# A transformer trunk on one core: two branches' weight sums move to VectorE, the last sums in HBM are issued one per product

## The chip, the core and the metric

The kernel runs on one core of one Trainium2 chip. The metric is the device time of one execution in microseconds (us); less is better. Engines: TensorE (PE; PEld is its weight load), VectorE (DVE), ScalarE (ACT), GpSimd (POOL) and SyncE (SP). SP issues the loads into on-chip memory; GpSimd issues the transfers that add in HBM.

## The reference

Sequence 512, width 1024, all in float32. One layer:

```python
h = _rmsnorm(x, norm_mix[l])
p = h @ w_in[l]
u, v, bg, cg, xb, zc, gl = jnp.split(p, splits, axis=-1)
ya = _sgu(gelu(u), gelu(v), sgu_ln[l], sgu_w[l], sgu_b[l])
yb = bg * _causal_dwconv(cg * xb, conv_b_w[l])
yc = _pool_mixer(zc, pool_w[l], pool_scale[l])
g = jax.nn.sigmoid(gl).reshape(bn, s, N_BRANCH, D_MODEL)
merged = (g[:, :, 0] * (ya @ w_br_a[l])
          + g[:, :, 1] * (yb @ w_br_b[l])
          + g[:, :, 2] * (yc @ w_br_c[l]))
x = x + merged @ w_o[l]
h = _rmsnorm(x, norm_ffn[l])
a = _causal_dwconv(h @ w_up[l], ffn_conv_w[l])
ag, av = jnp.split(a, 2, axis=-1)
x = x + (jax.nn.silu(ag) * av) @ w_down[l]
```

and a last RMSNorm. `w_in` is 1024 x 6144 (its last 3072 columns are the three gates), each `w_br` 512 x 1024, `w_up` 1024 x 5632, `w_down` 2816 x 1024. The change concerns the three products with `w_br` ("branches") and the three with the gates' columns ("gates").

## The kernel before

Precision: every float32 operand is cut into a high and a low part (`split`: a copy on ScalarE, line 59, and a subtraction on VectorE, line 67; lines 63 and 64 with the sign turned), and each product is three matmuls of 128x512 (`mm3`, lines 81 to 83).

Stages, in order of time: the `v` projection; the other projections of `w_in` (`u`, `z`, `cg`, `xb`, `bg`; tiles `pu` to `pbg`); then three times a branch and its gate (`bx0`, `gx0`, ...); the output product (`po`); the up projection (`pug`, `puv`); the down projection (`dx`, ...); the end.

Branches and gates are computed by a scheme with seven products of half-size blocks in place of eight: with quarters b11, b12, b21, b22 of the weights, M1 and M3 use b11 and b22, M2 uses b21, and M5, M6, M7, M4 use the sums t1 = b11+b12, t2 = b22+t1, t3 = b12+b22, t4 = b21+t2. A branch product has 12 matmuls, a gate product 24.

The sums of the weights are made in HBM: `WeightSums.copy` issues four copies, `add` four transfers that add into the copies; t2 waits for t1, and t4 for t2. All stand on GpSimd's queue in the order written (`in_order`): branch 0's copies as soon as a part of the first weights has landed (`pool_waits_for(wv_raw[3], "begun")`), then GpSimd's centering of `v`, then branch 0's adds, gate 0's copies and adds, branch 1's, gate 1's, branch 2's, gate 2's. A branch's transfers are 0.5 MB each, a gate's 1 MB.

Weights reach the chip in pieces of 128x1024 (512 KB). `Raws` keeps at most four loads under way or unsplit (`cap` 4): each freed buffer starts the next load on SP's queue (line 106), in the order of use. `Pieces` cuts each into one of four ring slots (`ring_hi`, `ring_lo`), so that three pieces stand cut ahead of the one that TensorE reads; a piece feeds 12 matmuls. Before the stage of the branches the ring is fed by `Cols` with two loads for each projection block of 48 matmuls.

An automatic scheduler sets each engine's instruction order when the program is built; an engine then works in that order and waits where an operand isn't there. One such order matters at the start: ScalarE's cast of `pw_raw` (a small weight, loaded on SP's queue) stands ahead of the last cast of `hT`.

Of the kernel before, what the change touches and what calls it, by code (L numbers as in the profile page):

```python
# [11 lines left out]
ALU = mybir.AluOpType  # L12
# [14 lines left out]
def trunk_kernel(  # L27
# [4 lines left out]
    nc = tc.nc  # L32
# [99 lines left out]
    class WeightSums:  # L134
        def __init__(self, name, b11, b12, b21, b22):
            t1, t2, t3, t4 = self.t = [
                dram.tile([P, b11.shape[1], 528], F32, name=f"{name}_t{i + 1}")[:, :, :512] for i in range(4)]
            self.base = [(t1, b11), (t3, b12), (t2, b22), (t4, b21)]
            self.added = [(t1, b12), (t3, b22), (t2, t1), (t4, t2)]

            self.products = (("m1", b11), ("m5", t1), ("m6", t2), ("m2", b21), ("m7", t3), ("m3", b22), ("m4", t4))

        def copy(self, n=4):
            for t, w in self.base[:n]:
# [8 lines left out]

    NEGATIVE = ("m1", "m4")

    def add_seven(name, weights, pieces):
        for m, w in weights.products:
            n = w.shape[1]
            for q in range(0, n, 2):
                add_block(f"{name}_{m}_{q}", w[:, q:min(q + 2, n)], pieces,  # L160
                          split_negative if m in NEGATIVE else split)

    def add_block(name, view, pieces, cut):
        raws.add(name, view)
# [180 lines left out]
    def quarters(half, c0):  # L345
        return [half(k)[:, :, c0 + 512 * h:c0 + 512 * h + 512] for k in range(2) for h in range(2)]

    gate_sums = [WeightSums(f"g{i}", *quarters(lambda k: w_in_v[:, 4 * k:4 * k + 4], 3072 + 1024 * i))
                 for i in range(3)]
    branch_sums = [WeightSums(f"br{i}", *quarters(lambda k: w_br_q[i][k], 0)) for i in range(3)]  # L350

    def pool_waits_for(t, name):

        in_order(nc.gpsimd.tensor_copy(tiny(name, name), t[:, 0:1]))

    pool_waits_for(wv_raw[3], "begun")
    branch_sums[0].copy()

    nc.vector.memset(ones_r.bitcast(F32), 1.0)
    eps_t = const.tile([P, 1], F32, name="eps_t")  # L360
# [220 lines left out]
        v_mm(t, 7)  # L581
        v_gelu(t)
    v_center()
    for i in range(3):
        branch_sums[i].copy()
        branch_sums[i].add()
        gate_sums[i].copy()
        gate_sums[i].add()

    raws.live = 0  # L590
    blocks = Cols(col_blocks[:n_in], slots)
# [164 lines left out]

    pieces = Pieces(slots)
    for i in range(3):
        add_seven(f"br{i}", branch_sums[i], pieces)
        add_seven(f"g{i}", gate_sums[i], pieces)  # L760

    for h in range(2):
        for k in (4, 6, 0, 2):
# [99 lines left out]
    def of_quarter(kh, r):  # L863
        return lambda k, i: [h[:, 4 * kh + k, 256 * r + P * i:256 * r + P * i + P] for h in hT]
# [6 lines left out]
    nrstd1 = small.tile([P, NT], F32, tag="nrstd", name="nrstd1")  # L871
    nc.vector.tensor_scalar(nrstd1, rstd1, -1.0, None, op0=ALU.mult)

    def product(o, st, n, first, last=True):

        for q in range(0, n, 2):
            [w] = pieces.take()
            for k in range(q, q + 2):
                mv = [p[:, 512 * (k - q):512 * (k - q) + 512] for p in w]
                for r in range(2):  # L880
                    mm3(o[r], st(k, r), mv, first and k == 0, k == n - 1, more=not first)
# [7 lines left out]
    def banks(name):  # L889
        return [bank(f"{name}{r}") for r in range(2)]  # L890
# [3 lines left out]
    def gate(i, c):  # L894
        def sigmoid(t, s, src, scale=rstd1):
            nc.scalar.activation(s, src, AF.Sigmoid, scale=scale[:, t:t + 1])

        def weigh(t, h, s):
            if i == 0:
                tt(c[t][h], s, c[t][h], ALU.mult)  # L900
            else:
                tt(s, s, c[t][h], ALU.mult)
                tt(acc[t][h], acc[t][h], s, ALU.add)

        x = banks(f"gx{i}")
        product(x, of_quarter(0, 0), 4, True)
        m1 = copies(0, f"m1{i}", x)
        d = banks(f"gd{i}")
        product(d, of_form(s1), 4, True)
        m5 = copies(1, f"m5{i}", d)  # L910
        product(x, of_form(s2), 4, False)
        m16 = copies(2, f"m16{i}", x)
        a = banks(f"ga{i}")
        product(a, of_quarter(1, 0), 4, True)
        for r in range(2):
            tt(m1[r], a[r], m1[r], ALU.subtract)
            sigmoid(r, m1[r], m1[r])
            weigh(r, 0, m1[r])
        product(x, of_form(s3), 4, False)
        if i == 2:  # L920
            for r in range(2):
                turn(r, 0)
        for r in range(2):
            tt(m5[r], x[r], m5[r], ALU.add)
            sigmoid(2 + r, m5[r], m5[r])
            weigh(2 + r, 1, m5[r])
        product(d, of_form(s4), 4, False)
        if i == 2:
            for r in range(2):
# [26 lines left out]
    def branch(i, form):  # L956
# [335 lines left out]
```

## Time and profile before

| | |
|---|---|
| median of 3 runs | 756.9 us (753.59 to 757.04) |
| profiled execution | 760.18 us, its span 758.4 us |
| TensorE busy | 728.3 us, 96% of the span |
| VectorE busy | 554.5 us, 73% |
| ScalarE busy | 367.9 us, 49% |
| GpSimd busy | 69.3 us, 9% |
| SP's DMA queue (q1) | 99.91 MB, 41.0% of 16 engines' span |
| GpSimd's DMA queue (q0) | 60.82 MB, 33.3% |

The span is the time from the first to the last instruction in the trace; the profiled execution's time is 1.8 us longer. A busy TensorE is not one at full pace: its matmuls overlap, so what it does is counted below in starts of matmuls. The times of the queues are shares of all 16 DMA engines together.

### The profile page before, as it was taken

Reading aid. Unit: us, or ns where it says so; the run is one execution under the profiler, and the core shown is the slowest. Engines: PE = TensorE matmul, PEld = TensorE weight load, DVE = VectorE, ACT = ScalarE, POOL = GpSimd, SP = SyncE. Lnnn points to the kernel's source line nnn. Section 1 sums busy time; section 2 is a strip of 40 time slices with the busy share of each in tenths; the row PEclk is TensorE's granted clock in tenths of the full one; section 3 lists DMA queues with packets and bytes.
Section 4 is the critical chain, followed back from the end, with each engine's and each line's share of the span. In section 5 each row is a group of like instructions: output and inputs, shape, how many; then the busy total and the mean of one; then the engine's idle time right before and its main releaser. Section 6 shows DMA issues by size and latency. Waiting matters only on the chain.

```text
span 758.4 us, 8935 instructions
## 1 busy us (share of the span) xinstructions
PE 728.3 (96%) x3258; PEld 595.7 (79%) x3258; DVE 554.5 (73%) x828; ACT 367.9 (49%) x540; POOL 69.3 (9%) x98
## 2 busy tenths in 40 slices
PE   8899999999987898999999999999999999999996
PEld 5688888887766666888888888888888888888885
DVE  6589899856474649759557776778777767998674
ACT  4555143254465456566344534344434443975454
POOL 1032111211221000000001101000000000000110
PEclk9999999999998999999999999999999999999999
DMA  7648999999999995766435999999923232476552
GB/s 257 246 121 208 316 248 271 268 307 271 308 278 364 261 277 180 220 204 216 151 92 177 205 311 228 312 212 301 242 87 109 84 112 72 142 232 218 183 167 111
DMA packets 94170, 162.40 MB, mean 214 GB/s; under 512 B 4359, under 2 KB 39599, under 8 KB 94127
## 3 DMA queue, kind: packets, MB, share of 16 engines
q1 hardware_dynamic: 70239, 99.91, 41.0%
q0 software_dynamic: 23168, 60.82, 33.3%
q10 hardware_dynamic: 720, 1.11, 0.4%
q8 instruction: 25, 0.41, 0.2%
q14 instruction: 18, 0.15, 0.1%
HBM read 159.73 MB, written 62.91 MB: 294 GB/s over the span
## 4 chain that ended last, share of the span: by engine, by line
PE 76%; DMA 16%; DVE 4%; ACT 1%; issue 1%; SPq 0%; ACTq 0%; DVEq 0%
DMA raw_g_m<-in_w_in_dram 6%; PE pug L81 5%; PE puv L81 5%; PE pug L83 5%; PE puv L83 5%; PE puv L82 5%; PE pug L82 5%; DMA raw_g_m<-g_t 4%; DMA raw_br_m<-in_w_br_b_dram 3%; PE dx L83 2%; PE dx L81 2%; PE po L81 2%; PE dx L82 2%; PE po L83 2%; PE po L82 2%; DVE ring_lo L67 2%
## 5 line engine op out<-in xcount | busy, mean ns | idle before, releaser
L81 PE MATMUL pug<-h2T_hi,ring_hi 128*128 128x512 f32 x176 | 68.7, 390 | 0.0
L83 PE MATMUL pug<-h2T_hi,ring_lo 128*128 128x512 f32 x176 | 68.5, 389 | 0.0
L82 PE MATMUL puv<-h2T_lo,ring_hi 128*128 128x512 f32 x176 | 68.5, 389 | 0.0
L81 PE MATMUL puv<-h2T_hi,ring_hi 128*128 128x512 f32 x176 | 68.5, 389 | 0.0
L82 PE MATMUL pug<-h2T_lo,ring_hi 128*128 128x512 f32 x176 | 68.5, 389 | 0.0
L83 PE MATMUL puv<-h2T_hi,ring_lo 128*128 128x512 f32 x176 | 68.5, 389 | 0.0
L67 DVE TENSOR_TENSOR ring_lo<-raw_g_m,ring_hi 128x1024 fp32r<-128x1024 f32 x30 | 36.5, 1224 | 42.4 <-ACT ring_hi L59 42.3
L59 ACT CAST ring_hi<-raw_g_m 128x1024 fp32r<-128x1024 f32 x30 | 31.3, 1052 | 43.0 <-DMA raw_g_m<-g_t 20.9
L59 ACT CAST ring_hi<-raw_ug 128x1024 fp32r<-128x1024 f32 x22 | 23.2, 1056 | 47.6 <-PE pug L82 42.3
L67 DVE TENSOR_TENSOR ring_lo<-raw_uv,ring_hi 128x1024 fp32r<-128x1024 f32 x22 | 26.9, 1221 | 25.1 <-ACT ring_hi L59 25.1
L67 DVE TENSOR_TENSOR ring_lo<-raw_d_m,ring_hi 128x1024 fp32r<-128x1024 f32 (+1 forms) x30 | 35.4, 1194 | 9.0 <-ACT ring_hi L59 8.9
L59 ACT CAST ring_hi<-raw_d_m 128x1024 fp32r<-128x1024 f32 (+1 forms) x30 | 29.4, 980 | 19.1 <-PE da L83 8.2
L83 PEld LDWEIGHTS pug<-h2T_hi,ring_lo 128*128 128x128 f32 x176 | 33.0, 188 | 7.0
L83 PEld LDWEIGHTS puv<-h2T_hi,ring_lo 128*128 128x128 f32 x176 | 33.0, 188 | 6.9
L81 PEld LDWEIGHTS puv<-h2T_hi,ring_hi 128*128 128x128 f32 x176 | 33.0, 188 | 6.9
L82 PEld LDWEIGHTS puv<-h2T_lo,ring_hi 128*128 128x128 f32 x176 | 33.0, 188 | 6.8
L82 PEld LDWEIGHTS pug<-h2T_lo,ring_hi 128*128 128x128 f32 x176 | 33.0, 188 | 6.8
L81 PEld LDWEIGHTS pug<-h2T_hi,ring_hi 128*128 128x128 f32 x176 | 33.0, 188 | 6.8
L67 DVE TENSOR_TENSOR ring_lo<-raw_ug,ring_hi 128x1024 fp32r<-128x1024 f32 x22 | 26.9, 1222 | 8.8 <-ACT ring_hi L59 8.8
L59 ACT CAST ring_hi<-raw_uv 128x1024 fp32r<-128x1024 f32 x22 | 23.2, 1054 | 19.2 <-PE puv L82 19.0
L1062 ACT ACTIVATE av<-av_y,colv 128x512 f32<-128x512 f32 x22 | 15.9, 724 | 27.9 <-DVE av_y L1060 26.9
L1162 POOL TENSOR_TENSOR xr<-xr,gain_f 128x512 f32<-128x512 f32 (+1 forms) x5 | 7.6, 1517 | 216.8 <-ACT sf L194 216.8
(426 smaller groups left out, 2037.4 us busy)
## 6 DMA issues: line engine op xcount, KB each, us to landing
g_t<-in_w_in_dram POOLq DMA_DIRECT2D x18, 1024.0 KB, 17.9
d_t<-in_w_down_dram POOLq DMA_DIRECT2D x6, 2816.0 KB, 27.9
raw_g_m<-g_t SPq DMA_DIRECT2D x24, 512.0 KB, 10.0
raw_ug<-in_w_up_dram SPq DMA_DIRECT2D x22, 512.0 KB, 5.5
raw_uv<-in_w_up_dram SPq DMA_DIRECT2D x22, 512.0 KB, 8.4
raw_d_m<-d_t SPq DMA_DIRECT2D x20, 512.0 KB, 4.0
raw_g_m<-in_w_in_dram SPq DMA_DIRECT2D x18, 512.0 KB, 9.7
raw_d_m<-in_w_down_dram SPq DMA_DIRECT2D x15, 512.0 KB, 3.4
```

The costliest lines, as they stand in the source:

```text
L59: return keep(nc.scalar.copy(hi, src))
L67: return keep(nc.vector.tensor_tensor(lo, src, hi.bitcast(F32), op=ALU.subtract))
L81: keep(nc.tensor.matmul(o, st[0], mv[0], start=first, stop=False, **skip))
L82: keep(nc.tensor.matmul(o, st[0], mv[1], start=False, stop=False, **skip))
L83: keep(nc.tensor.matmul(o, st[1], mv[0], start=False, stop=last, **skip))
L1062: nc.scalar.activation(a, y, AF.Copy, scale=ffn_w(2, c))
L1162: nc.gpsimd.tensor_tensor(y, y, gain3[h][:, cut], op=ALU.mult)
```

## The change

Four things change.

1. Branches 0 and 1 use no sums in HBM. The four quarters are loaded as they are and VectorE adds them in place (`add_branch`): 4 loads for 7 pieces, and 4 sums of 128x1024.
2. In each gate the products come in the order M1, M2, M6, M5, M7, M3, M4 in place of M1, M5, M6, M2, M7, M3, M4, and `branch_forms` of the next branch is written further ahead.
3. GpSimd's queue begins with gate 0's and gate 1's sums, behind the centering; the wait for `wv_raw` and branch 0's copies are gone.
4. The sums of branch 2 and gate 2 are cut into eleven steps (`behind`). Behind a product of a gate (and the third of branches 1 and 2) ScalarE copies one column of its result (`mark`), GpSimd copies that (`passed`), and issues the next step.

```diff
-            self.products = (("m1", b11), ("m5", t1), ("m6", t2), ("m2", b21), ("m7", t3), ("m3", b22), ("m4", t4))
+            self.products = {"m1": b11, "m2": b21, "m3": b22, "m4": t4, "m5": t1, "m6": t2, "m7": t3}
...
+    def add_branch(name, b11, b12, b21, b22, pieces):
+        blocks = [(f"{name}_b{n}", w) for n, w in ((11, b11), (12, b12), (22, b22), (21, b21))]
+        for block in blocks:
+            raws.add(*block)
...
+        def more(t, a):
+            nc.vector.tensor_tensor(t, t, a, op=ALU.add)
...
+        def m5(slot):
+            b11, b12 = need(2)
+            more(b11, b12)
+            split(*slot, b11)
+
+        def m6(slot):
+            b11, b12, b22 = need(3)
+            more(b11, b22)
+            split(*slot, b11)
+
+        def m2(slot):
+            b11, b12, b22, b21 = need(4)
+            split(*slot, b21)
+            more(b11, b21)
+            raws.free()
+
+        def m7(slot):
+            b11, b12, b22, b21 = got
+            more(b12, b22)
+            split(*slot, b12)
+            raws.free()
...
+        for source in (m1, m5, m6, m2, m7, m3, m4):
+            pieces.add(source)
...
-    branch_sums = [WeightSums(f"br{i}", *quarters(lambda k: w_br_q[i][k], 0)) for i in range(3)]
+    last_branch_sums = WeightSums("br2", *quarters(lambda k: w_br_q[2][k], 0))
...
-    pool_waits_for(wv_raw[3], "begun")
-    branch_sums[0].copy()
...
-    for i in range(3):
-        branch_sums[i].copy()
-        branch_sums[i].add()
-        gate_sums[i].copy()
-        gate_sums[i].add()
+    pool_waits_for(pw_raw, "begun")
+    for sums in gate_sums[:2]:
+        sums.copy()
+        sums.add()
...
-        add_seven(f"br{i}", branch_sums[i], pieces)
-        add_seven(f"g{i}", gate_sums[i], pieces)
+        if i < 2:
+            add_branch(f"br{i}", *quarters(lambda k: w_br_q[i][k], 0), pieces)
+        else:
+            add_seven(f"br{i}", last_branch_sums, (1, 5, 6, 2, 7, 3, 4), pieces)
+        add_seven(f"g{i}", gate_sums[i], (1, 2, 6, 5, 7, 3, 4), pieces)
...
+    behind = [lambda: last_branch_sums.copy()]
+    behind += [lambda: last_branch_sums.add(1)] * 4
+    behind += [lambda: gate_sums[2].copy(2)] * 2
+    behind += [lambda: gate_sums[2].add(1)] * 4
+
+    def next_sum(o):
+        if behind:
+            n = len(behind)
+            mark = tiny(f"mark{n}", f"mark{n}")
+            nc.scalar.copy(mark, o[:, 0:1])
+            pool_waits_for(mark, f"passed{n}")
+            behind.pop(0)()
...
         x = banks(f"gx{i}")
         product(x, of_quarter(0, 0), 4, True)
+        next_sum(x[1])
         m1 = copies(0, f"m1{i}", x)
-        d = banks(f"gd{i}")
-        product(d, of_form(s1), 4, True)
-        m5 = copies(1, f"m5{i}", d)
-        product(x, of_form(s2), 4, False)
-        m16 = copies(2, f"m16{i}", x)
         a = banks(f"ga{i}")
         product(a, of_quarter(1, 0), 4, True)
+        next_sum(a[1])
         for r in range(2):
             tt(m1[r], a[r], m1[r], ALU.subtract)
             sigmoid(r, m1[r], m1[r])
             weigh(r, 0, m1[r])
+        product(x, of_form(s2), 4, False)
+        next_sum(x[1])
+        m16 = copies(2, f"m16{i}", x)
+        if i < 2:
+            forms[i + 1] = branch_forms(i + 1)
+        d = banks(f"gd{i}")
+        product(d, of_form(s1), 4, True)
+        next_sum(d[1])
+        m5 = copies(1, f"m5{i}", d)
         product(x, of_form(s3), 4, False)
+        next_sum(x[1])
...
         product(x, form("s2"), 2, False)
+        if i > 0:
+            next_sum(x[1])
```

GpSimd's instructions at the start, before (`br_t` and `g_t` are the sums in HBM of a branch and a gate, `v` the tiles that it centers):

```order
L354 COPY begun<-wv_raw_96 128x1
L145 DMA br_t_125<-in_w_br_a_dram 256x1x512
L145 DMA br_t_127<-in_w_br_a_dram 256x1x512
L145 DMA br_t_126<-in_w_br_a_dram 256x1x512
L145 DMA br_t_128<-in_w_br_a_dram 256x1x512
L456 MEMSET ws_raw_172 64x4x64
L456 MEMSET ws_raw_173 64x4x64
L481 TENSOR_TENSOR v_205<-v_205,mu 128x512
```

The same place now:

```order
L506 MEMSET ws_raw_158 64x4x64
L506 MEMSET ws_raw_159 64x4x64
L531 TENSOR_TENSOR v_191<-v_191,mu 128x512
L531 TENSOR_TENSOR v_192<-v_192,mu 128x512
L531 TENSOR_TENSOR v_193<-v_193,mu 128x512
L531 TENSOR_TENSOR v_194<-v_194,mu 128x512
L407 COPY begun<-pw_raw 128x1
L146 DMA g_t_113<-in_w_in_dram 512x1x512
```

The four copies for branch 0 left the place ahead of the centering; the first transfer is now gate 0's copy behind it.

GpSimd from the end of gate 1's sums on, now (before, the same transfers of `br_t` and `g_t` stood there without the COPY rows):

```order
L151 DMA g_t_120<-g_t_118 512x512
L407 COPY passed_1643<-mark_1641 128x1
L146 DMA br_t_125<-in_w_br_c_dram 256x1x512
L146 DMA br_t_127<-in_w_br_c_dram 256x1x512
L146 DMA br_t_126<-in_w_br_c_dram 256x1x512
L146 DMA br_t_128<-in_w_br_c_dram 256x1x512
L407 COPY passed_1689<-mark_1687 128x1
L151 DMA br_t_125<-in_w_br_c_dram 256x1x512
L407 COPY passed_1732<-mark_1730 128x1
L151 DMA br_t_127<-in_w_br_c_dram 256x1x512
```

Each step of the last sums now stands behind a wait for one product's mark.

VectorE at the beginning of branch 1, before (`raw_br_m` are loaded pieces, `c`, `m` and `s` tiles of gate 0):

```order
L64 SCALAR_TENSOR_TENSOR ring_lo_78<-raw_br_m_0_1781,ring_hi_77 128x1024
L790 TENSOR_TENSOR m_1757<-gd_1687,m_1757 128x512
L790 TENSOR_TENSOR m_1758<-gd_1688,m_1758 128x512
L67 TENSOR_TENSOR ring_lo_80<-raw_br_m_0_1803,ring_hi_79 128x1024
L790 TENSOR_TENSOR c_1484<-m_1757,c_1484 128x512
L790 TENSOR_TENSOR c_1486<-m_1758,c_1486 128x512
L67 TENSOR_TENSOR ring_lo_82<-raw_br_m_0_1819,ring_hi_81 128x1024
```

The same place now (`raw_br_b` are the loaded quarters):

```order
L64 SCALAR_TENSOR_TENSOR ring_lo_78<-raw_br_b_1801,ring_hi_77 128x1024
L842 TENSOR_TENSOR m_1735<-gd_1781,m_1735 128x512
L178 TENSOR_TENSOR raw_br_b_1801<-raw_br_b_1801,raw_br_b_1826 128x1024
L842 TENSOR_TENSOR c_1444<-m_1735,c_1444 128x512
L842 TENSOR_TENSOR m_1736<-gd_1782,m_1736 128x512
L67 TENSOR_TENSOR ring_lo_80<-raw_br_b_1801,ring_hi_79 128x1024
L842 TENSOR_TENSOR c_1446<-m_1736,c_1446 128x512
L178 TENSOR_TENSOR raw_br_b_1801<-raw_br_b_1801,raw_br_b_1842 128x1024
L178 TENSOR_TENSOR raw_br_b_1826<-raw_br_b_1826,raw_br_b_1842 128x1024
```

The sums of the quarters (L178) stand between the cuts (L67) and the gate's multiplications (L842).

## Rows read from the trace of the kernel before

**Rows 1.** Stretch, us; busy PE, PEld, DVE, ACT, POOL (x count); clock, DMA share, GB/s.
```profile
178.55:224.09 45.54, 40.85 (x170) 30.91 (x168) 28.65 (x38) 24.02 (x31) 9.62 (x13) 1.00 1.03 292
224.09:251.29 27.20, 22.02 (x86) 17.38 (x84) 15.78 (x21) 14.74 (x22) 3.53 (x4) 0.87 1.06 328
251.29:295.45 44.16, 40.14 (x170) 31.13 (x168) 28.95 (x37) 22.16 (x29) 2.05 (x2) 1.00 0.91 249
295.45:317.13 21.68, 19.36 (x86) 15.69 (x85) 19.75 (x25) 14.13 (x19) 0.00 (x0) 1.00 0.69 214
317.13:356.99 39.86, 39.86 (x185) 33.19 (x184) 27.81 (x34) 24.69 (x33) 0.00 (x0) 1.00 0.67 207
```

**Rows 2.** Timeline of TensorE at the stage's two ends: start, us, what.
```profile
157.97 0.39 PE L81 MATMUL bx<-ring_hi,a 128*128 128x512 f32 x1
...
356.31 0.39 PE L81 MATMUL gx<-ring_hi,hT_hi 128*128 128x512 f32 x1
...
356.99 0.39 PE L81 MATMUL po<-ring_hi,mg_hi 128*128 128x512 f32 x1
```

**Rows 3.** The chain that ended last: start, us (a DMA's: issue to landing), what.
```profile
17.49 10.92 DMA pw_raw<-in_pool_w_dram
...
160.29 12.29 DMA raw_g_m<-in_w_in_dram
...
175.01 12.90 DMA raw_g_m<-g_t
...
239.80 13.69 DMA raw_g_m<-g_t
```

**Rows 4.** Groups of VectorE from 224 to 296 us: count, busy, mean ns, idle before.
```profile
L67 DVE TENSOR_TENSOR ring_lo<-raw_g_m,ring_hi 128x1024 fp32r<-128x1024 f32 x10 | 12.2, 1224 | 15.2 <-ACT ring_hi L59 15.2
L67 DVE TENSOR_TENSOR ring_lo<-raw_br_m,ring_hi 128x1024 fp32r<-128x1024 f32 x5 | 6.1, 1219 | 6.4 <-ACT ring_hi L59 6.4
L64 DVE SCALAR_TENSOR_TENSOR ring_lo<-raw_g_m,ring_hi 128x1024 fp32r<-128x1024 f32 x4 | 4.9, 1220 | 3.6 <-ACT ring_hi L63 3.6
...
L64 DVE SCALAR_TENSOR_TENSOR ring_lo<-raw_br_m,ring_hi 128x1024 fp32r<-128x1024 f32 x2 | 2.4, 1221 | 1.4 <-ACT ring_hi L63 1.4
```

**Rows 5.** DMA issues from 268 to 276.5 us: count, KB each, median us to landing.
```profile
raw_g_m<-g_t SPq DMA_DIRECT2D x3, 512.0 KB, 9.5
g_t<-g_t POOLq DMA_DIRECT2D x1, 1024.0 KB, 12.4
```

**Rows 6.** DMA issues from 300 to 345 us.
```profile
raw_g_m<-g_t SPq DMA_DIRECT2D x8, 512.0 KB, 3.6
```

**Rows 7.** Two stretches at the start, columns as in rows 1.
```profile
26.60:29.62 3.02, 0.03 (x1) 0.00 (x0) 0.01 (x1) 1.18 (x3) 0.30 (x1) 1.00 1.07 380
29.62:33.12 3.50, 3.50 (x8) 2.69 (x9) 3.10 (x6) 3.50 (x11) 0.00 (x0) 0.51 0.24 71
```

**Rows 8.** Timeline of ScalarE at the start; in brackets its idle time before.
```profile
28.44 0.62 ACT L59 CAST pw_hi<-pw_raw 128x512 fp32r<-128x512 f32 x1 [8.59 <-DMA pw_raw<-in_pool_w_dram]
```

**Rows 9.** The tile ws_raw: time to landing of the first of its loads.
```profile
DMA to landing us min/median/max: 2.8/2.8/2.8
```

**Rows 10.** Timeline of GpSimd: issues of its transfers, in brackets the idle time before.
```profile
16.64 2.94 POOL L145 DMA_DIRECT2D br_t<-in_w_br_a_dram  x4
...
26.85 0.30 POOL L456 MEMSET ws_raw<- 64x256 f32 x1 [6.95 <-DMA ws_raw<-in_sgu_w_dram]
...
53.55 2.16 POOL L150 DMA_DIRECT2D br_t<-in_w_br_a_dram  x2
...
69.25 3.36 POOL L145 DMA_DIRECT2D g_t<-in_w_in_dram  x4
...
111.01 1.08 POOL L150 DMA_DIRECT2D g_t<-g_t  x1 [12.74 <-issue]
111.64 3.27 POOL L145 DMA_DIRECT2D br_t<-in_w_br_b_dram  x4
```

**Rows 11.** The tile raw_bg (a projection's weights): time of its loads to landing.
```profile
DMA to landing us min/median/max: 14.8/21.3/25.0
```

More of the change, by code (lines that the diff above doesn't have):

```diff
@@ L154, in trunk_kernel, with add_seven @@
     NEGATIVE = ("m1", "m4")
-    def add_seven(name, weights, pieces):
-        for m, w in weights.products:
+    def add_seven(name, weights, order, pieces):
+        for m in (f"m{n}" for n in order):
+            w = weights.products[m]
             n = w.shape[1]
@@ L161, in add_seven, with need, m1, m3 @@
                           split_negative if m in NEGATIVE else split)
+    def add_branch(name, b11, b12, b21, b22, pieces):
+        blocks = [(f"{name}_b{n}", w) for n, w in ((11, b11), (12, b12), (22, b22), (21, b21))]
+        for block in blocks:
+            raws.add(*block)
+        got = []
+        def need(n):
+            while len(got) < n:
+                got.append(raws.get(blocks[len(got)][0]))
+            return got
+        def more(t, a):
+            nc.vector.tensor_tensor(t, t, a, op=ALU.add)
+        def m1(slot):
+            split_negative(*slot, need(1)[0])
+        def m5(slot):
[16 more added lines that the diff above has]
+            raws.free()
+        def m3(slot):
+            split(*slot, got[2])
+            raws.free()
+        def m4(slot):
+            split_negative(*slot, got[0])
+            raws.free()
+        for source in (m1, m5, m6, m2, m7, m3, m4):
+            pieces.add(source)
     def add_block(name, view, pieces, cut):
@@ L872, in trunk_kernel, with product @@
     nc.vector.tensor_scalar(nrstd1, rstd1, -1.0, None, op0=ALU.mult)
-    def product(o, st, n, first, last=True):
+    behind = [lambda: last_branch_sums.copy()]
[9 more added lines that the diff above has]
+            behind.pop(0)()
+    def product(o, st, n, first):
         for q in range(0, n, 2):
@@ L927, in gate @@
         product(d, of_form(s4), 4, False)
+        next_sum(d[1])
         if i == 2:
@@ L934, in gate @@
             weigh(r, 1, m16[r])
-        if i < 2:
-            forms[i + 1] = branch_forms(i + 1)
         product(x, of_quarter(1, 1), 4, False)
+        next_sum(x[1])
         for r in range(2):
@@ L965, in branch @@
         product(x, form("s2"), 2, False)
+        if i > 0:
+            next_sum(x[1])
         m16 = copies(2, f"bm16{i}", x)
@@ L1188, in trunk_kernel @@
     pieces = Pieces(slots)
-    add_seven("d", down_sums, pieces)
+    add_seven("d", down_sums, (1, 5, 6, 2, 7, 3, 4), pieces)
     def taken(qs):
```

## The prediction

> **What bounds the kernel now.** I read the busy time by stretches first. TensorE is the busiest engine of the table above, so only its idle or slowed time can be won. In the stretches of the branch and gate products [rows 1] it idles 45.5 − 40.9 = 4.7 us, then 5.2, 4.0 and 2.3; the third gate idles nothing. The second branch also ran at a granted clock of 0.87. To count both at once I take the stage's length: from the first branch product (157.97) to the first output product (356.99) [rows 2] is 199.0 us. A matmul starts 0.227 us after the one before it (three in 0.68 us) [rows 2]. Three branches have 7 products of 12 matmuls, three gates 7 of 24: 756 matmuls, 171.4 us. The third gate, which waits for nothing, takes 39.9 us for 38.1 us of matmuls, so the transposes in it are 1.8. The floor is 173.2, and the stage loses **25.8 us**.
>
> Next, the chain that ended last. Between 160 and 282 us it is a circle: a weight load of 12 to 14 us, its two halves cut by ScalarE and VectorE, and then the next load into the buffer that this freed. One circle takes 14.7 us (160.29 to 175.01), or 16.1 where the load is one of 13.69 and the cuts are the same 2.4 [rows 3]. Four buffers go round in it, so a piece of weights comes every 3.7 to 4.0 us; TensorE uses one in 12 × 0.227 = 2.72. The cuts agree: 21 pieces in the 72 us from 224 to 296 [rows 4], 3.43 us each. Why the loads are slow: with one sum of 1 MB in flight they take 9.5 us [rows 5]; when none is, 3.6 [rows 6]. The loads are slowed by the sums in HBM, the last of which, issued in the stretch of [rows 5], lands some 12.4 us later, at 281.
>
> Last, the start. From 26.6 to 29.6 us TensorE is idle and for the 3.5 us behind that its clock is 0.51 [rows 7]: 3.0 + 1.7 = **4.7 us**. ScalarE stood 8.59 us for pw_raw [rows 8], a load of 256 KB that took 10.92 us [rows 3]; the cast of hT, which TensorE needs, is queued behind it.
>
> **The change, part by part.**
>
> *Branch 0's copies leave the start.* The four copies that the "begun" of wv_raw set off just before pw_raw's load are gone. Of ws_raw's two loads of the same size the one issued before the copies landed in 2.8 us [rows 9]; for the other, issued after the copies (16.64), GpSimd waited until 26.85 [rows 10]. pw_raw, issued at 17.49, may land as late as 25.3 without a stall (TensorE runs dry at 26.6; two casts of 0.62 us stand between [rows 8]). I take the whole 4.7; the bounds are 0 (it is late for another reason) and 4.7. GpSimd's next work, the centering, starts where it did relative to the products.
>
> *The order of the sums.* The first two gates' sums now start behind the centering: at 53.55 before [rows 10], some 48.9 after. The first gate's took 42.4 us from its copies (69.25) to the next family's (111.64), and the last add is issued 41.8 us in; with 12.4 us for it [rows 5] the second gate's end at 48.9 + 42.4 + 41.8 + 12.4 = 145.5. The stage begins at 157.97 − 4.7 = 153.3. So branch 0 and the first gate product (until 177.7) see no sum in flight, where before the circle was already slow at 160. The cover for this is the projection stage, whose TensorE never waits before 158 although the loads there already take 14.8 to 25.0 us [rows 11].
>
> *Branches 0 and 1.* 16 transfers in HBM of 0.5 MB and 6 of the stage's 63 loads vanish. In exchange VectorE gets 4 sums of 128x1024 for each branch. No such sum is in the trace; the nearest row, the cut of the same shape, is 1.22 us [rows 4]. So 4.9 us in each branch of 19.0 us, beside seven cuts (8.5 us). Bounds: 0 on the path if they fit into the time in which VectorE waits for ScalarE, 9.8 if every one lies on it. I take 0: three pieces are cut ahead, 8 us of cover, and the waits of ring_lo alone are 15.2 us in 72 [rows 4]. Without that cover the price is 9.8. Behind a waiting sum on VectorE stand the gate's multiplications, and TensorE waits for none of them directly.
>
> *The last sums, behind marks.* Gate 0 runs from 172.3, a product takes 5.44 us, gate 0 ends at 210.4, gate 1 starts at 229.4. The eleven marks fall at 177.7, then every product, at 218.6 in branch 1, and the last at 245.7. The last two adds wait for one another: 240.3 + 12.4 + 12.4 = 265. The third gate wants its first sum 10.9 us behind its start (286.5), and a load ahead of that; 20 us are to spare. In the 87 us from 177.7 to 265 TensorE can use 32 pieces; four of branch 1's loads make seven of them, so 29 loads are wanted. At 3.43 us each 25.4 come; three pieces are cut ahead and up to four loads have landed by then: 28.4 to 32.4. Missing: 0.6 loads at most, **2 us**. At the slow circle's 4.0 us each and three pieces ahead 4.2 loads are missing, 17 us. Bounds 0 and 17; I take 2, since adds now come apart and 3.43 is a mean over a stretch with three 1 MB transfers queued. The marks: 11 copies of one column on ScalarE, each below the 0.62 us of 512 columns [rows 8], so 0 to 6.8; they stand next to copies that wait for the same product, hence 0.
>
> A rule weighs against this. Rows first: one sum in flight gives loads of 9.5 us [rows 5], several 12.3 to 13.7 [rows 3], none 3.6 [rows 6], so issuing one at a time gives back only a third. The Trainium skill, "DMA: Bandwidth & Descriptors", section "Queues, rings and completion order", says that every DMA engine takes turns between the queues that have work, a packet at a time. By it a lone sum takes as many turns as a queued one, and only the pauses help; that is the first rival below, and by it the term of 2 us would be 17. The rows lie between.
>
> *M2 second, branch forms earlier.* The same matmuls in another order: M1 and M2 read weights as they are, so two more pieces come before the first sum is wanted; and the subtraction from M2's product comes 11 us earlier for VectorE, which was busy 19.75 of 21.7 us in the third branch [rows 1]. Counted as 0.
>
> **The sum** goes against the profiled execution, 760.2 us: 760.2 − 4.7 − 25.8 + 2 = 731.7. The runs shown have a median 3.3 us below it; part of that is starvation, which varies and is gone afterwards, so I subtract half: **730 us**.
>
> **Rivals.**
> 1. *The sums still starve the loads*: gates 0 and 1 at the slow circle, 17 us instead of 2: 745. For it: the queue is hardly ever empty from 177.7 to 265, since an add of 12.4 us is longer than a product of 5.44. Against: the loads start with a full lead and are six fewer.
> 2. *VectorE becomes the bound*: all eight sums on the path: 730 + 9.8 = 740. For it: 19.75 of 21.7 us; against: that was the backlog of a starvation that ended at 282.
> 3. *The other side: the projections starve.* From 49 to 145 us gate sums now follow without a pause, while each projection of 10.9 us takes two loads. Four buffers allow 4 × 5.44 − 2.3 = 19.5 us for a load (2.3 for its two cuts); before, loads took 14.8 to 25.0 [rows 11] in spells. If all 12 loads of these stages took 25, it costs 12 × 5.5 / 4 = 16.5 us, 746. At 28.5 us for every one it eats the whole gain, and from 30 on the kernel is slower.
> 4. *The start doesn't change* (pw_raw late all the same): 730 + 4.7 = 735.
> 5. *The change does nothing*: sums shift to other places and the loads starve as before; 757.
>
> **How the numbers follow.** My forecast 0.67 with its own range 725 to 736; rival 1 0.11, 2 0.07, 3 0.05 (0.03 of it slower than before), 4 0.06, 5 0.04. The range from 724 to 744 holds the forecast, rivals 2 and 4 and about half of 1. One half per cent, 3.8 us, is what a measurement of this kernel tells from no change. Faster: all but rival 5 and the worse part of 3, 0.93; same 0.04; slower 0.03.
>
> **What would show it.** The start: no TensorE gap near 26 us, no clock of 0.5 behind it, pw_raw landing before 25. The stage: from the first bx to the first po some 175 us, loads of about 4 us up to 178 and from 5 to 10 between 178 and 265, no starved clock. GpSimd: the second gate's last add issued near 133. The sums on VectorE: 1.2 us each. Wrong if TensorE waits for ring_lo in gates 0 and 1 with loads of 12 us (rival 1), if VectorE is busy without a gap through branch 1 (2), or if pcg, pxb and pbg show gaps (3).

## The result and the profile after

The changed kernel takes 736.2 us (median of 4 runs, 735.38 to 737.91) where the kernel before took 757.0 beside it (4 runs, 753.59 to 759.44): a ratio of 0.973, 95% interval 0.969 to 0.977. The forecast was 730, its range 724 to 744. The profiled execution took 736.67 us, its span is 734.9.

First the stage of branches and gates, TensorE at its two ends (start, us, what):

```profile
152.66 0.39 PE L81 MATMUL bx<-ring_hi,a 128*128 128x512 f32 x1
...
333.57 0.39 PE L81 MATMUL po<-ring_hi,mg_hi 128*128 128x512 f32 x1
```

It begins 5.3 us earlier than in [rows 2] and is 180.9 us long, where it was 199.0 and 173.2 is the floor. So 18.1 us came from the stage and 5.3 from ahead of it, and **7.7 us are still lost** in the stage. The stretches from gate 0 to branch 2, cut at the first matmul of each, say where (columns as in [rows 1]):

```profile
171.70:209.78 38.08, 38.08 (x170) 31.53 (x168) 27.21 (x37) 23.52 (x35) 11.82 (x16) 1.00 0.95 274
209.78:231.98 22.20, 19.94 (x86) 15.53 (x84) 19.81 (x26) 16.23 (x26) 4.23 (x5) 1.00 1.04 323
231.98:270.06 38.08, 38.08 (x170) 31.53 (x168) 27.75 (x35) 20.03 (x30) 4.01 (x6) 1.00 1.03 270
270.06:293.71 23.65, 20.94 (x86) 16.83 (x85) 19.08 (x23) 15.16 (x20) 0.00 (x0) 0.93 0.70 220
```

A gate without a wait is 168 × 0.2267 = 38.1 us, and gates 0 and 1 are just that; they were 45.5 and 44.2. A branch without a wait is 84 × 0.2267 = 19.0. Branch 0 (152.66 to 171.70) is that; branch 1 is 22.2, 3.2 too long, and branch 2 is 23.65, 4.6 too long, part of it at a lower clock (0.93). The whole loss is in these two (gate 2 takes 39.9, as before).

The start. ScalarE's cast, in brackets its wait, and then the two stretches of [rows 7], moved ahead by the 5.3 us:

```profile
22.95 0.63 ACT L59 CAST pw_hi<-pw_raw 128x512 fp32r<-128x512 f32 x1 [3.52 <-DMA pw_raw<-in_pool_w_dram]
```
```profile
21.29:24.31 3.02, 3.02 (x15) 2.51 (x14) 0.18 (x1) 1.36 (x3) 0.00 (x0) 1.00 0.99 322
24.31:27.81 3.50, 3.50 (x17) 2.92 (x16) 3.09 (x6) 3.50 (x11) 0.00 (x0) 1.00 0.55 176
```

The cast starts 5.5 us earlier than in [rows 8], TensorE is busy all through, and the clock of 0.51 is gone.

The DMA issues of three stretches (count, KB each, median us to landing): 155 to 178 us, 182 to 194, 240 to 250:

```profile
raw_g_m<-g_t SPq DMA_DIRECT2D x5, 512.0 KB, 3.5
raw_g_m<-in_w_in_dram SPq DMA_DIRECT2D x4, 512.0 KB, 3.5
...
raw_g_m<-in_w_in_dram SPq DMA_DIRECT2D x2, 512.0 KB, 11.8
br_t<-in_w_br_c_dram POOLq DMA_DIRECT2D x2, 512.0 KB, 10.1
raw_g_m<-g_t SPq DMA_DIRECT2D x2, 512.0 KB, 9.2
...
g_t<-in_w_in_dram POOLq DMA_DIRECT2D x1, 1024.0 KB, 11.1
raw_g_m<-g_t SPq DMA_DIRECT2D x2, 512.0 KB, 9.3
raw_g_m<-in_w_in_dram SPq DMA_DIRECT2D x2, 512.0 KB, 13.0
```

Where no sum is in flight a load takes 3.5 us, as in [rows 6]; in the stretches beside branch 2's sums of 0.5 MB and gate 2's of 1 MB it takes 9 to 13, as in [rows 3, 5], where the prediction had said 5 to 10. So the marks did not make a load beside the sums much faster. They did not always keep the sums apart either: the add in the last of the three stretches is issued at 239.88 and takes 11.1 us, and the next is issued at 243.75. Still the 17 us of the first rival did not come: the kernel can live through a good part of the slow loads.

The rule that the prediction set against the change is that of the Trainium skill, "DMA: Bandwidth & Descriptors", section "Queues, rings and completion order": each DMA engine goes round the queues that have work, a packet at a time. The loads of 9 to 13 us agree with what the prediction drew from it, that spacing the sums does little for a load beside one; no row here shows the turns themselves.

When sums are issued (GpSimd's timeline): gate 1's last add, then the first of branch 2 and the last of gate 2.

```profile
132.77 1.02 POOL L151 DMA_DIRECT2D g_t<-g_t  x1 [12.56 <-issue]
...
177.89 2.81 POOL L146 DMA_DIRECT2D br_t<-in_w_br_c_dram  x4
...
206.83 1.55 POOL L146 DMA_DIRECT2D g_t<-in_w_in_dram  x2
...
259.36 1.02 POOL L151 DMA_DIRECT2D g_t<-g_t  x1 [10.31 <-issue]
```

And when weights are loaded (SyncE's timeline; the second number of a row is the time over which its issues are spread):

```profile
124.25 11.11 SPq L106 DMA_DIRECT2D raw_br_b<-in_w_br_a_dram  x4
155.77 3.00 SPq L106 DMA_DIRECT2D raw_g_m<-in_w_in_dram  x2
...
195.87 8.36 SPq L106 DMA_DIRECT2D raw_br_b<-in_w_br_b_dram  x4
218.53 5.57 SPq L106 DMA_DIRECT2D raw_g_m<-in_w_in_dram  x4
```

The gaps matter below: from 135.4 to 155.8 us no load is issued, and none from 204.2 to 218.5, while the four quarters of branch 0 and branch 1 hold the four buffers until VectorE has added and cut them.

What a slow load does is seen at the end of gate 1, where ScalarE's cuts wait for them (in brackets how long):

```profile
251.45 1.06 ACT L59 CAST ring_hi<-raw_g_m 128x1024 fp32r<-128x1024 f32 x1 [2.29 <-DMA raw_g_m<-g_t]
...
255.63 1.06 ACT L59 CAST ring_hi<-raw_g_m 128x1024 fp32r<-128x1024 f32 x1 [3.13 <-DMA raw_g_m<-in_w_in_dram]
...
259.13 1.05 ACT L59 CAST ring_hi<-raw_g_m 128x1024 fp32r<-128x1024 f32 x1 [1.48 <-DMA raw_g_m<-in_w_in_dram]
```

TensorE does not wait for these pieces, they were ahead of it. It waits 12 us later, in branch 2; the chain that ended last there (start, us, what):

```profile
270.04 1.06 ACT ring_hi L59
271.13 1.23 DVE ring_lo L67
...
277.10 0.62 DVE c L842
277.74 0.60 ACT bm L951
278.37 0.65 PE bx L81
```

In the piece left out VectorE does the gate's last sums and weightings and one more cut, in one heap; behind them stands the copy `bm`, which must read a bank (the memory that TensorE adds into) before the next product adds into it, and TensorE stood 2.7 us for it.

In branch 1 VectorE works from 205.6 to 224.9 us without a wait, its four sums among the rest. Then it waits itself, 2.26 us for the cut of a piece of gate 1:

```profile
227.16 1.23 DVE L64 SCALAR_TENSOR_TENSOR ring_lo<-raw_g_m,ring_hi 128x1024 fp32r<-128x1024 f32 x1 [2.26 <-ACT ring_hi L63]
```

The chain that ended last there:

```profile
217.25 1.23 DVE raw_br_b L178
218.53 7.46 DMA raw_g_m<-in_w_in_dram
226.07 1.07 ACT ring_hi L63
...
228.31 0.70 DVE c L842
...
229.14 0.47 PE bx L81
```

It runs through both suspects. The last sum on VectorE (L178) frees a quarter's buffer; only then can gate 1's first load start, which takes 7.46 us (3.5 with no sum in flight); and the branch's own subtraction `c`, for which TensorE stands 1.7 us, is behind the cut of that piece in VectorE's order. A VectorE that is busy without a gap through branch 1 was the sign that the prediction named for its second rival (VectorE becomes the bound). It came for the first 15 of the branch's 22.2 us, and whether VectorE is the cause the rows can't tell: an engine that gets its input late and in a heap is full too. So that was the first question to the chip.

### The profile page after: what moved, and what is told of

The parts are those of the page before. It is cut to its first block, busy times and chain, and to the rows that moved or that the text cites. A ratio compares the mean times of both kernels' runs of the same rounds, so it can differ in the third digit from the quotient of the medians.

```text
span 734.9 us, 8928 instructions
## 1 busy us (share of the span) xinstructions
PE 720.7 (98%) x3258; PEld 594.8 (81%) x3258; DVE 562.7 (77%) x836; ACT 370.6 (50%) x551; POOL 62.6 (9%) x93
## 4 chain that ended last, share of the span: by engine, by line
PE 93%; DVE 3%; DMA 2%; ACT 1%; issue 1%; SPq 0%; ACTq 0%
PE pug L83 5%; PE puv L83 5%; PE pug L81 5%; PE puv L81 5%; PE puv L82 5%; PE pug L82 5%; PE gx L82 3%; PE gx L81 3%; PE gx L83 3%; PE dx L83 2%; PE dx L82 2%; PE po L81 2%; PE dx L81 2%; PE po L83 2%; PE po L82 2%; PE gd L83 1%
## 5 line engine op out<-in xcount | busy, mean ns | idle before, releaser
L67 DVE TENSOR_TENSOR ring_lo<-raw_g_m,ring_hi 128x1024 fp32r<-128x1024 f32 x30 | 36.6, 1224 | 29.2 <-ACT ring_hi L59 29.1
L67 DVE TENSOR_TENSOR ring_lo<-raw_uv,ring_hi 128x1024 fp32r<-128x1024 f32 x22 | 26.9, 1222 | 25.1 <-ACT ring_hi L59 25.1
L67 DVE TENSOR_TENSOR ring_lo<-raw_d_m,ring_hi 128x1024 fp32r<-128x1024 f32 (+1 forms) x30 | 35.8, 1204 | 9.0 <-ACT ring_hi L59 8.9
L59 ACT CAST ring_hi<-raw_d_m 128x1024 fp32r<-128x1024 f32 (+1 forms) x30 | 29.5, 982 | 18.6 <-PE da L83 8.2
L67 DVE TENSOR_TENSOR ring_lo<-raw_ug,ring_hi 128x1024 fp32r<-128x1024 f32 x22 | 26.9, 1222 | 8.8 <-ACT ring_hi L59 8.7
L1136 ACT ACTIVATE ag<-ag_y,colv 128x512 f32<-128x512 f32 x22 | 15.8, 720 | 21.5 <-DVE ag_y L1134 21.5
```

What stands on the lines that cost most here:

```text
L59: return keep(nc.scalar.copy(hi, src))
L67: return keep(nc.vector.tensor_tensor(lo, src, hi.bitcast(F32), op=ALU.subtract))
L1136: nc.scalar.activation(a, y, AF.Copy, scale=ffn_w(2, c))
```

## The experiments

Two theories at first. **V**: the sums on VectorE are on the path, and it is the bound in the branches. **D**: the loads that the last sums in HBM slow are the price, and VectorE is only where it shows. Each kernel ran on one chip in turn with the kernel before; a ratio is to that one, with its 95% interval. Runs 1 to 4, 5 to 8 and 9 to 12 were on three different chips, so medians of different groups are compared by their ratios, and places by the losses in the traces.

All losses below are worked out in one way: the start of the first matmul of a branch or gate to that of the next, less 19.04 us for a branch, 38.08 for gates 0 and 1; the whole stage (first bx to first po) less 173.2. Each rests on one trace.

**1. The start alone, in the kernel before.**

```diff
-    pool_waits_for(wv_raw[3], "begun")
-    branch_sums[0].copy()
...
     v_center()
+    pool_waits_for(pw_raw, "begun")
```

> The kernel before with one edit: branch 0's copies leave the start, all sums stand behind the centering in the old order. Theory S (the copies delayed pw_raw's load, and ScalarE stood in front of it): TensorE's gap at 26.6 us and the half clock behind it go, 5 us less, 752; the stage of the branches keeps its loss of about 26 us. Rival (the gap has another cause, or branch 0's sums now come too late): 757 or more.

755.9 us, ratio 0.998 (0.996 to 1.000), between the two numbers: 1.6 us of the 5.3 are left. The start did change: the stage begins at 152.68. But it is 201.7 us long, so 28.5 are lost in it and not 25.8; its end:

```profile
354.37 0.39 PE L81 MATMUL po<-ring_hi,mg_hi 128*128 128x512 f32 x1
```

Half of the start's gain was handed back by this trace, and more by the medians. GpSimd issues the last sum at 269.0 us, where it was 268.7 before (the four copies now stand in the row of the sums), which fits a stage that begins earlier and only waits longer. The 5.3 us are worth their size only together with the rest of the change.

**2. Without the eight sums on VectorE.**

```diff
         def more(t, a):
-            nc.vector.tensor_tensor(t, t, a, op=ALU.add)
+            pass
```

> The changed kernel without the eight sums on VectorE: M5, M6, M7 and M4 of branches 0 and 1 read quarters that are not added up. Theory V (VectorE, busy without a gap from 200 to 225 us, costs branch 1 its 3.1 us): branch 1 loses nothing, 733 us; branch 2 keeps its 4.6. Theory D (slow loads cost it, VectorE only waits behind them): branch 1 loses 2 to 3 us all the same, 736.

737.2 us, ratio 0.973 (0.970 to 0.975): nothing gained. Branch 1 lost 0.7 us only (it is 19.70 long), but gate 1 then lost 2.7 and branch 2 lost 6.7:

```profile
209.73:229.43 19.70, 19.29 (x86) 15.69 (x85) 14.04 (x18) 12.53 (x21) 4.22 (x5) 1.00 1.02 324
229.43:270.18 40.75, 39.13 (x170) 31.34 (x168) 28.62 (x38) 21.50 (x31) 4.60 (x6) 1.00 1.00 260
270.18:295.92 25.74, 22.47 (x86) 17.65 (x84) 19.79 (x25) 15.15 (x20) 0.00 (x0) 0.87 0.68 221
```

Branch 1 did as V said, and the whole as D said: what branch 1 won was asked for again further on. So VectorE's sums have a part in where the loss falls due, but they are not the price. Against V as the bound.

**3. Without the last sums in HBM**, the marks kept: each step is taken from the list and not issued. Branch 2 reads its plain quarters and gate 2 the sums of gate 1, as many loads of the same size as before.

```diff
+            b11, b12, b21, b22 = quarters(lambda k: w_br_q[2][k], 0)
+            last_branch_sums.products = {f"m{n + 1}": b for n, b in enumerate((b11, b21, b22, b12, b21, b22, b12))}
...
-        add_seven(f"g{i}", gate_sums[i], (1, 2, 6, 5, 7, 3, 4), pieces)
+        add_seven(f"g{i}", gate_sums[min(i, 1)], (1, 2, 6, 5, 7, 3, 4), pieces)
...
-            behind.pop(0)()
+            behind.pop(0)
```

> The changed kernel without the last sums in HBM: branch 2 reads plain quarters and gate 2 reads gate 1's sums, the marks and GpSimd's copies of them stay. Theory D: loads take 4 us through the whole stage and the losses of branches 1 and 2 (7.7 us) go, 729 us. Theory V: branch 1 keeps its 3.1 us, 732; if VectorE alone makes branch 2's loss too, 736.

729.3 us, ratio 0.962 (0.959 to 0.965). The stage is 173.15 us (153.51 to 326.66): nothing is lost, with all eight sums still on VectorE and all eleven marks in place. So the last sums cost some 7 us, the marks by themselves nothing, and 729.3 is what the kernel takes with the stage at its floor. As D said.

**4. Without marks**: the last sums right behind gate 1's.

```diff
-    for sums in gate_sums[:2]:
+    for sums in (*gate_sums[:2], last_branch_sums, gate_sums[2]):
...
-    behind = [lambda: last_branch_sums.copy()]
-    behind += [lambda: last_branch_sums.add(1)] * 4
-    behind += [lambda: gate_sums[2].copy(2)] * 2
-    behind += [lambda: gate_sums[2].add(1)] * 4
+    behind = []
```

> The changed kernel with the last sums right behind gate 1's on GpSimd's queue, without marks: they run from about 132 to 230 us in place of 178 to 270. If the pace is what keeps the loads fed, gates 0 and 1 starve again as before, 745 us. Theory D in its other form (it matters only when sums are in flight, not how many): the contention moves to branch 0 and gate 0, branch 2 loses nothing, 732 to 738.

742.2 us, ratio 0.979 (0.976 to 0.982): above D's 732 to 738, nearer to the 745 of the other. Gate 0 lost 7.4 us, branch 1 lost 4.1, the rest nothing. So the marks are worth some 4 us in this kernel (3.7 by the losses of the stage, 4.5 by the ratios), and the loss has moved to where the sums went. The place agrees with D in that branch 2 loses nothing, and not in branch 0, which loses nothing either. D does not say yet when a slow load costs something. The next four were to find that out.

**5. Only branch 2's sums ahead**, unmarked; gate 2's stay marked and so move up, to the products at which branch 2's were.

```diff
-    for sums in gate_sums[:2]:
+    for sums in (*gate_sums[:2], last_branch_sums):
...
-    behind = [lambda: last_branch_sums.copy()]
-    behind += [lambda: last_branch_sums.add(1)] * 4
-    behind += [lambda: gate_sums[2].copy(2)] * 2
+    behind = [lambda: gate_sums[2].copy(2)] * 2
```

> The changed kernel with one edit: branch 2's four sums in HBM are issued unmarked right behind gate 1's, and only gate 2's six steps stay behind marked products. The sums then lie in two spells, one from about 132 us and one from about 180 us on, and the loads may refill the ring of raw pieces between them. Theory D (what is lost is slow loads beside the last sums, 7 us): less of them overlap with any one stretch of the gates, so 730 to 733 us. Rival (the loss only moves, to branch 0 and gate 0, as it did when all marks were gone): 736 us or more, with TensorE waits of 2 to 3 us each in gate 0.

739.8 us, ratio 0.977 (0.974 to 0.980). D's number missed, the rival's came, though not where the rival put the loss. Branch 2's sums (issued from 133.8 to 159.7 us) cost nothing: branch 0 and the first half of gate 0 lose nothing. But gate 2's, now from 178.2 to 223.1, cost 3.8 us in gate 0 and 7.3 in branch 1.

**6. Branch 2 on VectorE too**, gate 2's steps marked as in 5.

```diff
-        if i < 2:
-            add_branch(f"br{i}", *quarters(lambda k: w_br_q[i][k], 0), pieces)
-        else:
-            add_seven(f"br{i}", last_branch_sums, (1, 5, 6, 2, 7, 3, 4), pieces)
+        add_branch(f"br{i}", *quarters(lambda k: w_br_q[i][k], 0), pieces)
```

> The changed kernel with branch 2's four sums taken out of HBM and added on VectorE like those of branches 0 and 1; gate 2's six steps stay behind marked products. Four transfers of 1 MB that cost the loads are gone, and VectorE has four more sums of 1.1 to 1.2 us each. Theory D (slow loads): about 730 us. Rival V (VectorE's backlog in branch 2 is the price): the third branch's 4.9 us of sums lie on the chain there, 736 us or more.

739.4 us, ratio 0.977 (0.974 to 0.980), where D said 730 and V 736 or more. V's number came and its place did not: branch 2 itself loses 0.2 us with its four sums on VectorE. Gate 0 loses 2.1 and branch 1 loses 8.0, much as in 5: eight transfers fewer (four copies and four additions, of 0.5 MB each and not of the expectation's 1 MB), and no gain.

**7. The old order of products in the gates**, with the forms read where they were before.

```diff
-        add_seven(f"g{i}", gate_sums[i], (1, 2, 6, 5, 7, 3, 4), pieces)
+        add_seven(f"g{i}", gate_sums[i], (1, 5, 6, 2, 7, 3, 4), pieces)
...
```

> The changed kernel with the gates' products in the order of before (M2 third from the end of the first half, as the old table has it) and the forms that branches read back in their old place; VectorE sums and marks stay. If the order of the gates carries part of the gain, 739 us or more with TensorE waits where M2's operand or its sums come late; if it carries none, 736 to 737 us.

739.5 us, ratio 0.976 (0.973 to 0.979). The stage loses 10.7 us against 7.7, spread over gates 0 and 1 and branches 1 and 2. The intervals of the two ratios overlap, so that M2 second is worth some 3 us is what the one trace shows, and not settled.

**8. As 6, but gate 2's sums unmarked**, right behind gate 1's, 44 us earlier.

```diff
-    for sums in gate_sums[:2]:
+    for sums in gate_sums:
...
+    behind = []
```

> As the run with branch 2's sums on VectorE, and gate 2's sums too are issued unmarked, right behind gate 1's. Theory D: half as many transfers meet the loads of branch 0 and gate 0 as when all marks were gone (742 us), so 731 to 736 us; with marks the same kernel should be 730 us. If the marks were what matters and not the number of sums, 740 us or more. Rival V gives 736 us or more for both.

**730.1 us**, ratio 0.964 (0.961 to 0.967): faster than the changed kernel, whose interval lies above, and within a microsecond of run 3. Gate 0, branch 1 and branch 2:

```profile
171.97:210.18 38.21, 38.21 (x170) 31.45 (x168) 32.10 (x43) 25.25 (x33) 1.01 (x1) 1.00 0.85 251
210.18:229.28 19.10, 19.10 (x85) 15.76 (x84) 18.89 (x24) 15.31 (x23) 0.00 (x0) 1.00 0.50 157
...
267.36:286.65 19.29, 19.29 (x85) 15.61 (x84) 18.89 (x22) 12.60 (x17) 0.00 (x0) 1.00 0.46 140
```

V falls for good: VectorE makes twelve sums here, is busy 18.89 of 19.10 us in branch 1, and TensorE does not wait. But the loads are not fast either. Its DMA issues from 160 to 177.5 us:

```profile
raw_g_m<-g_t SPq DMA_DIRECT2D x3, 512.0 KB, 10.6
raw_g_m<-in_w_in_dram SPq DMA_DIRECT2D x2, 512.0 KB, 13.7
```

and its GpSimd:

```profile
133.80 3.43 POOL L146 DMA_DIRECT2D g_t<-in_w_in_dram  x4
...
179.96 1.01 POOL L151 DMA_DIRECT2D g_t<-g_t  x1 [15.05 <-issue]
```

The same sums of gate 2 cost 10.3 us of stage when they are issued from 178.1 to 221.6 (run 6) and 0.4 from 133.8 to 180.0. This gave **theory P**: what counts is beside which loads a sum lies. Its two halves: from 135 to 156 us no load is issued, so a sum there slows nothing; and gate 0 starts with its pieces cut and its buffers loaded, so it stands some slow loads. Late in gate 0 they are used up, and branch 1, which wants four new loads and four sums at once, pays. The last four tried this.

**9. Branch 0 back in HBM**, copies at the start as before, its additions ahead of gate 0's sums.

```diff
+    pool_waits_for(wv_raw[3], "begun")
+    first_branch_sums.copy()
...
-    pool_waits_for(pw_raw, "begun")
+    first_branch_sums.add()
     for sums in gate_sums[:2]:
...
-        if i < 2:
+        if i == 1:
```

> The changed kernel with branch 0's part undone: its four sums are made in HBM as before, with the copies at the kernel's start and the additions ahead of gate 0's, and branch 0 reads seven pieces. Theory (the start gains 5.3 us because these copies are gone, and sums that lie in the projections cost nothing as such): the start's 5.3 us are lost again, and gate 1's sums end some 10 us later than 144 us, in the stretch up to 156 us in which no load is issued; so 742 us, stage of branches and gates as in the changed kernel (181 us). Rival (the copies at the start are hidden, and the start's gain has another source): 736 to 737 us.

740.5 us, ratio 0.979 (0.975 to 0.982); the profiled stage begins at 157.07 and is 179.9 us long. The cast stands at the start as it did in [rows 8]:

```profile
27.25 0.62 ACT L59 CAST pw_hi<-pw_raw 128x512 fp32r<-128x512 f32 x1 [7.59 <-DMA pw_raw<-in_pool_w_dram]
```

and from 26.60 to 29.62 us TensorE is again busy for 1.18 us only. So the start's gain comes from these copies: 4.4 us of it went with them. The stage's loss is 6.7 us where it was 7.7.

This kernel says two things more. Branch 0 reads seven pieces here, so its loads are issued from 129.1 us on without the pause, beside gate 1's sums (last add issued at 158.95). Issues from 129 to 150 us:

```profile
raw_br_m<-in_w_br_a_dram SPq DMA_DIRECT2D x3, 512.0 KB, 11.8
raw_br_m<-br_t SPq DMA_DIRECT2D x3, 512.0 KB, 13.4
```

Yet branch 0 and gate 0 lose nothing. So a pause of the loads isn't needed for an early sum to be free, and the first half of P is not what decides. And with the last sums behind the same marks as in the changed kernel, branch 1 loses 5.1 us and branch 2 only 1.6: how the loss divides between the two is not fixed by the place of the sums alone.

**10. Gate 2's sums early, branch 2's marked as in the changed kernel.**

```diff
-    for sums in gate_sums[:2]:
+    for sums in gate_sums:
...
     behind += [lambda: last_branch_sums.add(1)] * 4
-    behind += [lambda: gate_sums[2].copy(2)] * 2
-    behind += [lambda: gate_sums[2].add(1)] * 4
```

> The changed kernel with gate 2's sums issued unmarked right behind gate 1's (134 us to about 192 us); branch 2's steps stay behind the same marked products of gate 0 (178 to 212 us). Theory P (what counts is beside which loads a sum lies: free while the loads pause, from 135 to 156 us, costly beside a gate's loads): branch 2's loss of 4.6 us is gone and branch 1's of 3.2 us stays or grows a little since gate 2's last sum now meets it, 732 to 735 us. Rival N (the number of sums in HBM counts, wherever they lie): 736 to 737 us.

738.0 us, ratio 0.976 (0.972 to 0.979): above what P said, and near the rival's number. The stretches say otherwise than the rival, though. Branch 2's loss is gone as P had it; gate 0 (42.41) loses 4.3 us and branch 1 (23.70) 4.7:

```profile
171.38:213.79 42.41, 40.03 (x170) 31.22 (x168) 28.67 (x38) 24.64 (x36) 11.10 (x14) 1.00 1.06 312
213.79:237.49 23.70, 21.26 (x85) 16.80 (x84) 22.20 (x28) 16.72 (x24) 0.00 (x0) 0.93 0.51 148
```

Gate 2's sums here lasted into gate 0 (the last is issued at 176.7), and branch 2's followed at once (180.6 to 210.6). The first spell by itself costs 0.4 us (run 8), the second some 3 (branch 1 in the changed kernel); joined they cost 9. I had added them up.

**11. Branch 2 on VectorE, gate 2's steps behind the very products of the changed kernel.**

```diff
-    behind = [lambda: last_branch_sums.copy()]
-    behind += [lambda: last_branch_sums.add(1)] * 4
+    behind = [lambda: None] * 5
```

> The changed kernel with branch 2's sums on VectorE, and gate 2's six steps behind the very products behind which the changed kernel has them (207 to 270 us). Theory P: branch 1's loss of 3.2 us goes with the transfers beside gate 0, and branch 2's loss of 4.6 us stays, as gate 2's sums still lie beside gate 1's loads: 733 to 735 us. Rival N: 730 us, as for the run with the same sums unmarked. Rival V (VectorE): more than 737 us.

733.7 us, ratio 0.971 (0.967 to 0.974), as P said. Branch 1 loses 0.6 us and branch 2 still 3.9:

```profile
209.88:229.50 19.62, 19.32 (x85) 15.69 (x84) 17.15 (x23) 14.37 (x24) 4.55 (x5) 1.00 1.02 314
...
267.58:290.53 22.95, 20.31 (x85) 15.38 (x84) 22.58 (x27) 14.38 (x19) 0.00 (x0) 1.00 0.44 144
```

So by this run most of the 3.2 us in branch 1 came from branch 2's sums beside gate 0's loads, and most of the 4.6 in branch 2 from gate 2's beside gate 1's. One trace says so, and run 9, with both families of sums where the changed kernel has them, divides its loss otherwise.

**12. As 6, with one mark for all six steps.**

```diff
-    behind = [lambda: gate_sums[2].copy(2)] * 2
-    behind += [lambda: gate_sums[2].add(1)] * 4
+    behind = [last_sums]
```

> As the run with branch 2's sums on VectorE and gate 2's steps marked (739.4 us), but one mark only, at gate 0's first product; the other five steps follow as fast as the queue issues them, so that the sums lie at the same place (from 178 us). Theory P (the place counts, not the marks): 738 to 741 us, lost at the end of gate 0 and in branch 1. Rival M (the marks themselves cost, being waits between the steps): 730 to 732 us.

741.3 us, ratio 0.980 (0.977 to 0.984), at the upper end of what P said. Gate 0 loses 1.4 and branch 1 loses 9.8. Five marks fewer gain nothing, as all eleven cost nothing in run 3 and as the prediction had counted; what the marks do is place the sums.

Together (us lost in the profiled execution; the spells are those of GpSimd's issues, from first to last):

| kernel | branch 2's sums | gate 2's sums | gate 0 | branch 1 | gate 1 | branch 2 |
|---|---|---|---|---|---|---|
| changed | 177.9–205.1 | 206.8–259.4 | 0 | 3.2 | 0 | 4.6 |
| 3 | none | none | 0 | 0 | 0 | 0 |
| 9 | 182.3–208.9 | 211.2–264.8 | 0 | 5.1 | 0 | 1.6 |
| 8 | VectorE | 133.8–180.0 | 0.1 | 0.1 | 0 | 0.3 |
| 11 | VectorE | 206.0–256.7 | 0 | 0.6 | 0 | 3.9 |
| 6 | VectorE | 178.1–221.6 | 2.1 | 8.0 | 0 | 0.2 |
| 12 | VectorE | 178.3–221.9 | 1.4 | 9.8 | 0 | 0.3 |
| 5 | 133.8–159.7 | 178.2–223.1 | 3.8 | 7.3 | 0 | 0 |
| 4 | 132.5–159.3 | 159.9–207.3 | 7.4 | 4.1 | 0 | 0 |
| 10 | 180.6–210.6 | 132.3–176.7 | 4.3 | 4.7 | 0 | 0 |

Read down the last columns: the loss lies in the later part of the gate beside which the sums ran, and in the branch behind it. A spell whose last sum is issued by 180 costs nothing, unless another follows at once (4 and 10).

## Why the prediction was right, and where it was off

**The bound and the 25.8 us.** Right: the stage was the place, and the floor of 173.2 us was reached in run 3 (173.15). What the change takes out of it is 18.1 us. The time, 736.2, lies just outside the forecast's own 725 to 736, and inside 724 to 744, a range made wide for rivals of which none came as it stood.

**The start, 4.7.** Right in cause and size: 5.3 us measured, and given up again when the copies came back (run 9). What the prediction did not say: with the stage as it was before, the gain would have been handed back in part (run 1).

**The order of the first sums.** Right: the second gate's last add was to be issued near 133 and was at 132.77, and the loads issued from 155 to 178 us took 3.5 us.

**The sums on VectorE, 0 of 0 to 9.8.** Right. They last 1.22 us each, as the nearest row said:

```profile
L178 DVE TENSOR_TENSOR raw_br_b<-raw_br_b,raw_br_b x8: 1216/1221/1226, 141.4 to 217.2; 128x1024 f32<-128x1024 f32 x8
```

The second rival's sign came for most of branch 1 (VectorE full to 224.9 us) and its cause did not: run 2 took the sums away and gained nothing on the whole, run 8 made four more and lost next to nothing (0.4 us in the stage). The sign was badly chosen, since a late engine is full too. One thing the prediction left out: the sums also hold the buffers, and so the next loads, until they are done.

**The projections** (third rival): false. The loads of `raw_bg` took 16.8, 18.2 and 18.6 us (lowest, median, highest; 14.8, 21.3 and 25.0 in [rows 11]), and TensorE waits in none of `pcg`, `pxb` and `pbg`.

**The last sums, 2 of 0 to 17.** This is the step that was off, by 5.7 us, with its mechanism right (the sums slow the loads, and the pieces in hand cover part of it). It took 3.43 us for each load from 177.7 to 265 us, 25.4 loads, and set them against 29 wanted with the lead of the cut and loaded pieces as one store for the whole 87 us. The supply was judged well: 26 loads are issued in that stretch (19 for gates, 7 for branches), one in 3.36 us. The store was not, as far as the rows tell. Branch 1 stops the loads for 14 us (none is issued from 204.2 to 218.5), and wants four loads and four sums close together; it pays there, behind gate 0 with its slow loads, and branch 2 pays behind gate 1. So I looked for the loss in gates 0 and 1, which lose nothing, and it was in branches 1 and 2: 3.2 + 4.6.

**M2 second, 0.** Open: one trace says 3 us (run 7), the times don't part it from nothing.

**From the profiled run to the median, −1.7.** Wrong, by itself 1.2 us: the profiled run after is 0.5 us above its median. 760.2 − 5.3 − 25.8 + 7.7 = 736.8, and the profiled run took 736.7, so the sum closes; of the 6.2 us by which 736.2 lies above 730, the residual has 5.7 and this 1.2, less 0.6 for the start (0.1 is rounding).

What stays open is why a spell from 134 to 180 costs nothing. That no load is issued for 20 us of it is in the rows, but run 9 has no such pause and loses nothing there either; that the stage begins with full buffers and lives on them is argued from slow loads that cost nothing (10.6 and 13.7 us in run 8, 11.8 and 13.4 in run 9). No run varied the number of pieces in hand. Nor is it shown how the loss comes to be divided between branches 1 and 2.

## What to carry to other kernels

A transfer that slows others is not priced by its length alone but by what the others need meanwhile: try background transfers ahead of the stretch that needs many loads, while its buffers are still full, rather than spread over that stretch (here the same sums of gate 2 cost 0.4 us early, 4.4 and 10.3 when spread: runs 8, 11 and 6). Don't count the pieces in hand as one store for a long stretch: look for the stage that holds the buffers or wants several loads at once, since in the changed kernel the loss showed there and not in the gates beside which the loads were slow. An engine that is busy without a gap next to a waiting one is only a suspect until its work has been taken away once; here it passed a delay on.

## What the runs showed of the hardware that was not expected

A sum of half the size does not halve what a load beside it loses. Beside branch 2's sums of 0.5 MB (the changed kernel, 182 to 194 us) the loads' medians were 11.8 and 9.2 us, against 3.5 with no sum in flight; beside gate 2's of 1 MB, in the same stretch of run 6, they were:

```profile
raw_g_m<-in_w_in_dram SPq DMA_DIRECT2D x2, 512.0 KB, 12.7
raw_g_m<-g_t SPq DMA_DIRECT2D x2, 512.0 KB, 13.9
```

Run 6 also has more sums in flight at once there, so that size and number are not told apart.
